# z of the softmax heads as seven block products of two by two, and six plain products moved in front of v

## The chip, the cores and the metric

The kernel runs on one core of a Trainium2 chip. The metric is the device time of one execution in microseconds; what is given is the median of several. A profiled execution is one single execution, with its own time.

## What is computed

The reference is one decoder layer on x of 512 rows and 1024 columns, all in float32. Cut to what matters here:

```python
h = rms_norm(x, norm_w)
qa, ka, va, za, qb, kb, vb, zb, gl_a, gl_b = split(h @ w_in)    # 8 of 512 columns, 2 of 1024
qa, ka = rms_norm(heads(qa), q_norm_w), rms_norm(heads(ka), k_norm_w)
oa = moba_attention(qa, ka, heads(va), rel_bias)                # softmax heads, branch a
ob = stick_breaking_attention(heads(qb), heads(kb), heads(vb))  # branch b
ya = (merge(oa) * silu(za)) @ w_up_moba
yb = (merge(ob) * silu(zb)) @ w_up_sb
y = sigmoid(gl_a + gb_a) * ya + sigmoid(gl_b + gb_b) * yb
x = x + y @ w_out
```

The z of the title is `za`, the gate path of the softmax heads; q and k are `qb` and `kb` of the stick-breaking heads; v is `va` and `vb` together.

## The kernel before

**Numbers.** Every large matrix product is made of three matmuls (`mm3`, L237): each operand is split into a rounded high part and the low remainder, and low times high, high times low and high times high are added up. Of a weight block of 128x1024 (512 KB), ScalarE writes the high part (L194) and VectorE the low part (L196); the raw block lies in one of three `wr` buffers, the parts in one of three `wh` and `wl` buffers. `load_w` (L157) hands out the next block of a fixed list, `stream` (L107), and keeps three of them ahead, so a block's split is written into the buffers of the block three before.

**Seven products in place of eight.** v, q and k (not z) are computed by a 2x2 block scheme of the Strassen-Winograd kind: x is cut into four quarters, and so are the weights; seven products of quarters give the result. For it some products take sums of x's quarters, S1 to S4 (`mix_x`, L368: VectorE sums, ScalarE high part, VectorE low part), and sums of the weights' blocks, T1 to T4 (`TERMS`, L38). Those sums are made by DMA: `load_sum` (L118) brings one block into a tile of the "v" pool, `add_sum` (L128) lets a DMA issued by POOL add a second block to it. T2 is T1 plus a block, T4 is T2 plus a block. The blocks "11", "21" and "22" are plain blocks that need no sum; by the list `ORDER` (L102) q and k take 11, T1, 21, T2, 22, T3, T4. The products of `columns` (L750) give q and k transposed, with matmuls of 256 columns; those of `values` (L701) give v, with matmuls of 512 columns, two blocks a product. PSUM banks X, D, Z, Y and E take the products; X collects several. Copies by ScalarE and sums by VectorE (L764) put the quarters of the result together.

**Order of the work around the change.** TensorE does, one after the other: qa; ka; `FRONT` (L46), that is a gate chunk g:0 and four z chunks (`f_z`, L640, `chunk_ct`, L505: 24 matmuls of 512 columns over one weight block); v; q; k; then the attention, in whose steps the list `FILLS` (L47) puts further gate, zb and up chunks. Beside the front, VectorE and ScalarE square and norm ka (`head_norm`, L401), spread qa and ka over the heads (`head_rows`, L415), turn them (`flip`, L437: eight VectorE transposes, eight DMAs by SP to memory), bring them back (`fetch`, L451: four DMAs by POOL), and split them inside v (`split_flipped`, L462).

**What sets the order.** A scheduler puts each engine's instructions into one fixed order, by the place in the program and by when it takes them to be ready; at run time each engine works through its order. `tc.issue_after(ins)` pins what follows on the engine of `ins` behind it, in order only. SP's and POOL's DMA issues are such orders too. Tiles of a pool are shared: "v" has 9 of 128x1024, "g" 31 of 128x512, PSUM has six banks "s" and two "pj".

Of the kernel before, what the change touches and what calls it, by code (L numbers as in the profile page):

```python
# [16 lines left out]
P = 128  # L17
# [28 lines left out]
FRONT = ("g:0", "za:0", "za:1", "za:2", "za:3")  # L46
# [13 lines left out]
def hybrid_layer(ctx: ExitStack, tc: tile.TileContext, x, xT, w, rel, out):  # L60
# [41 lines left out]
    ORDER = dict.fromkeys("qk", ("11", "T1", "21", "T2", "22", "T3", "T4"))  # L102
    ORDER["v"] = "11", "T1", "T2", "22", "T3", "21", "T4"
    HALVES = {"v": "ab", "q": ("",), "k": ("",)}
    BASE = {"v": 8, "q": 16, "k": 20}
    BLOCKS_OUT = [(kind, b + h) for kind in "vqk" for b in ORDER[kind] for h in HALVES[kind]]
    stream = list(range(8)) + list(range(24, 24 + len(FRONT))) + BLOCKS_OUT + list(range(24 + len(FRONT), WO)) + OUT  # L107

    def block(name, kind):
        if kind in "qk":  # L110
# [59 lines left out]

    def fetch_w(c):
        cuts = ((0, 512), (512, 1024)) if c < 2 else ((0, 1024),)
        item = stream[c]
        if item in sums:
# [62 lines left out]
    def mm3(ps, aH, aL, bH, bL, start, stop, on=False):  # L237

        with tc.issue_after(guard[0]) if guard[0] and start else nullcontext():
            T.matmul(ps, aH, bL, start=start, stop=False, skip_group_check=on)  # L240
# [127 lines left out]
    def mix_x(k):  # L368

        a, b = xraw[k], xraw[k + 4]  # L370
        left, right = slice(0, HS), slice(HS, S)
        V.tensor_tensor(b[:, right], a[:, right], b[:, right], op=ALU.subtract)
        V.tensor_tensor(a[:, right], a[:, left], a[:, right], op=ALU.subtract)
        V.tensor_tensor(a[:, left], b[:, right], a[:, left], op=ALU.subtract)
        V.tensor_tensor(b[:, left], b[:, left], a[:, left], op=ALU.add)
        h = tp.tile([P, 4 * PQ], F32R, tag="pt", bufs=4, name=f"mx{k}")
        if k < 2:
            l = tp.tile([P, 4 * PQ], F32R, tag="turned", bufs=2, name=f"ml{k}")
            l = [l[:, n * S:(n + 1) * S] for n in range(2)]
        else:  # L380
            l = [tp.tile([P, S], F32R, tag=("p3", "sx")[n], bufs=2, name=f"ml{k}{n}") for n in range(2)]
        for n, raw in enumerate((a, b)):
            hi, lo = h[:, n * S:(n + 1) * S], l[n]
            A.activation(hi, raw, AF.Copy)
            V.tensor_tensor(lo, raw, hi.bitcast(F32), op=ALU.subtract)
            for cs, name in ((left, ("S2", "S4")[n]), (right, ("S3", "S1")[n])):
                mixed[name, k] = hi[:, cs], lo[:, cs]
# [27 lines left out]
    def head_rows(ps, name, st):  # L415
        rows = []
        for t in range(NT):
            n = slot(f"{name}n{t}")
# [43 lines left out]
    def split_flipped(raws, name):  # L462

        res = []
        for p, raw in enumerate(raws):
# [18 lines left out]

    def spread(ps, name):
        with tc.issue_after(low[count[0] - 2]):
            rows = head_rows(ps, name, st[name])
        flipped[name] = flip(rows, name)

    flipped, raws = {}, {}  # L490
# [174 lines left out]

    for i, word in enumerate(FRONT):
        kind, n = word.split(":")
        f_g(int(n)) if kind == "g" else f_z("a", int(n))
        if i == 0:
            norm(ps_ka, "ka", after=summed[0])  # L670
            mix_x(0)
        elif i == 1:
            mix_x(1)
            summed.append(each(add_sum, "v", ("T3",), last["ka"]))
        elif i == 2:
            bring("qa")
            mix_x(2)
        elif i == 3:
            spread(ps_ka, "ka")
            mix_x(3)  # L680
        elif i == 4:
            bring("ka")
# [12 lines left out]
    s1, s2, s3, s4 = ([mixed[f"S{n}", k] for k in range(4)] for n in (1, 2, 3, 4))  # L695
# [5 lines left out]
    def values():  # L701
# [6 lines left out]
        X, W, Y = ([bank("s", f"v{n}{t}") for t in range(2)] for n in "xwy")  # L708
# [3 lines left out]
        product(W, s1, True)  # L712
        chain((load_sum, "q", "T1"), (add_sum, "q", "T1"))
        product(X, s2, False)
# [3 lines left out]
        chain((add_sum, "v", "T4"))  # L718
        for t in range(2):
            V.tensor_tensor(v_of["b"][t], W[t], top[t], op=ALU.subtract)  # L720
        qa.extend(split_flipped(raws["qa"], "qa"))
        product(Y, s4, True)
        for t in range(2):
            V.tensor_tensor(v_of["b"][t], Y[t], v_of["b"][t], op=ALU.add)
        product(X, s3, False)
        for t in range(2):
            A.activation(low_b[t], X[t], AF.Copy)
        for t in range(2):
            V.tensor_tensor(v_of["b"][2 + t], W[t], low_b[t], op=ALU.subtract)
        chain((load_sum, "q", "T2"), (add_sum, "q", "T2"), (load_sum, "q", "T3"), (add_sum, "q", "T3"))  # L730
        ka.extend(split_flipped(raws["ka"], "ka"))
        Z = [bank("s", f"vz{t}") for t in range(2)]
        product(Z, a12, True)
        for t in range(2):
            V.tensor_tensor(v_of["a"][t], Z[t], v_of["a"][t], op=ALU.add)
        product(X, a22, False)
# [6 lines left out]
    def product_ct(ps, a, start):  # L743
        hi, lo = load_w()
        for n in range(2):
            for k in range(4):
                ks = slice((2 * k + n) * P, (2 * k + n + 1) * P)
                mm3(ps[:, n * HS:(n + 1) * HS], hi[:, ks], lo[:, ks], *a[k], start and n + k == 0, k == 3, True)

    def columns(kind, c_of, steps):  # L750

        def quarter(c, r):
            return [c_of[2 * c + n][:, r * HS:(r + 1) * HS] for n in range(2)]

        def half_of(a, n):
            return a[n] if isinstance(a, list) else a[:, n * HS:(n + 1) * HS]

        def copy(ps, dst):
            for n in range(2):
                A.activation(dst[n], half_of(ps, n), AF.Copy)  # L760

        def add(dst, a, b, op=ALU.add):
            for n in range(2):
                V.tensor_tensor(dst[n], half_of(a, n), half_of(b, n), op=op)  # L764

        q11, q21, q12, q22 = (quarter(c, r) for c in range(2) for r in range(2))
        X, D, Z, Y, E = (bank("s", f"{kind}{n}") for n in "xdzye")
        product_ct(X, a11, True)
        copy(X, q11)
        product_ct(D, s1, True)  # L770
        copy(D, q22)
        steps[2]()
        product_ct(Z, a12, True)
        add(q11, Z, q11)
        product_ct(X, s2, False)
        add(q12, q22, X, ALU.subtract)
        steps[4]()
        product_ct(Y, s4, True)
        add(q12, Y, q12)
        product_ct(X, s3, False)  # L780
        add(q22, q22, X, ALU.subtract)
        copy(X, q21)
        steps[6]()
# [298 lines left out]
```

## Time and profile before

| what | us |
|---|---|
| median of 3 runs (382.64 to 383.13) | 382.86 |
| the profiled execution | 382.79 |
| its span, first to last instruction | 380.9 |
| VectorE busy, of the span | 292.2 |
| ScalarE busy, of the span | 216.8 |
| first z chunk to first matmul of v | 54.92 to 76.68 |
| v | 76.68 to 114.76 |
| q and k, to the first scores | 114.76 to 155.16 |

Times within the trace count from the span's start. PE is TensorE's matmuls, PEld its weight loads, DVE is VectorE, ACT is ScalarE, POOL is GpSimd and SP the engine that mostly issues DMAs. A row of the timeline gives start and duration, engine, line, the tiles written and read, and in brackets how long the engine was idle before it and what ended that. A row of a window gives the sum and, for each engine, the busy time in it; behind these stand TensorE's granted clock, the DMA engines' share and GB/s.

### The profile page before, as it was taken

How to read it: one execution, taken by the hardware profiler on the slowest of the kernel's cores; microseconds unless marked ns; L12 is line 12 of the kernel's file. 1: busy time of each engine (PE TensorE's matmuls, PEld its weight loads, DVE VectorE, ACT ScalarE, POOL GpSimd, SP SyncE). 2: the span in 40 equal slices, each digit the busy share in tenths (PEclk: the TensorE clock that was granted, in tenths of full speed). 3: DMA queues.
4: the chain of work that ended last, by engine and by line, in shares of the span. 5: the costliest groups of instructions: out<-in, count | busy, mean ns of one | idle time of the engine just before them, and what ended most of it. 6: DMA issues, size and time to landing. Idle time of an engine off the chain costs nothing.

```text
span 380.9 us, 5678 instructions
## 1 busy us (share of the span) xinstructions
PE 376.3 (99%) x2007; PEld 311.0 (82%) x2007; DVE 292.2 (77%) x505; ACT 216.8 (57%) x380; POOL 82.7 (22%) x125
## 2 busy tenths in 40 slices
PE   8999999999999999999999999999999999999996
PEld 5888888888889999888787878787878877888885
DVE  4828998975894656788885669599999717999962
ACT  5675655555875453799757464775464304368530
POOL 3859959213011020000000003001000000430310
PEclk9999999999999999999999999999999999999999
DMA  7989898989887994565998384959799853699964
GB/s 256 346 339 331 222 198 300 246 265 256 228 231 228 263 216 114 175 177 175 304 367 295 116 268 132 281 172 286 223 297 278 255 234 111 163 267 290 166 159 171
DMA packets 37611, 89.53 MB, mean 235 GB/s; under 512 B 4040, under 2 KB 16840, under 8 KB 37584
## 3 DMA queue, kind: packets, MB, share of 16 engines
q1 hardware_dynamic: 29856, 61.90, 47.8%
q0 software_dynamic: 6720, 23.09, 27.0%
q10 hardware_dynamic: 1008, 4.19, 3.2%
q8 instruction: 15, 0.25, 0.2%
q14 instruction: 12, 0.10, 0.1%
HBM read 70.27 MB, written 14.70 MB: 223 GB/s over the span
## 4 chain that ended last, share of the span: by engine, by line
PE 99%; DVE 0%; issue 0%
PE gl L240 8%; PE gl L242 8%; PE gl L241 8%; PE poa L627 2%; PE pob L627 2%; PE sb L525 2%; PE sa L525 2%; PE zb L240 2%; PE yb L240 2%; PE ka L240 2%; PE zb L241 2%; PE yb L242 2%; PE yb L241 2%; PE zb L242 2%; PE ya L240 2%; PE vx L242 2%
## 5 line engine op out<-in xcount | busy, mean ns | idle before, releaser
L196 DVE TENSOR_TENSOR wl<-wr,wh 128x1024 fp32r<-128x1024 f32 (+1 forms) x60 | 70.9, 1182 | 20.4 <-ACT wh L194 20.2
L194 ACT ACTIVATE wh<-wr 128x1024 fp32r<-128x1024 f32 (+1 forms) x60 | 61.7, 1030 | 24.6 <-issue 7.8
L240 PE MATMUL gl<-xl,wh 128*128 128x512 f32 x128 | 50.3, 393 | 0.0
L241 PE MATMUL gl<-xh,wl 128*128 128x512 f32 x128 | 49.8, 389 | 0.0
L242 PE MATMUL gl<-xh,wh 128*128 128x512 f32 x128 | 49.8, 389 | 0.0
L657 ACT ACTIVATE gl<-gl,x 128x512 f32<-128x512 f32 x16 | 10.9, 684 | 33.8 <-PE gl L242 33.8
L240 PEld LDWEIGHTS gl<-xl,wh 128*128 128x128 f32 x128 | 24.0, 188 | 5.3 <-ACT wh L194 0.2
L242 PEld LDWEIGHTS gl<-xh,wh 128*128 128x128 f32 x128 | 24.0, 188 | 5.1
L241 PEld LDWEIGHTS gl<-xh,wl 128*128 128x128 f32 x128 | 24.0, 188 | 4.9
L547 ACT ACTIVATE pa<-pa,m 128x512 f32<-128x512 f32 (+3 forms) x32 | 17.6, 551 | 8.3 <-DVE m L545 8.3
L146 POOL COPY turn_of<-pta 1x1 f32<-1x1 f32 x1 | 2.1, 2064 | 85.8 <-DVE sx L582 85.8
L572 DVE TENSOR_TENSOR_SCAN sx<-om,begin 128x512 f32<-128x512 f32 (+1 forms) x16 | 16.8, 1075 | 0.0
L594 DVE STREAM_TRANSPOSE turneda<-pa 128x384 f32<-128x384 f32 (+1 forms) x24 | 13.4, 600 | 2.2 <-ACT pa L552 2.0
L545 DVE CUSTOM_DVE_ANT_0 pa<-sa,om 128x512 f32<-128x512 f32 (+3 forms) x32 | 13.8, 483 | 0.6 <-DMA om<-e_dr 0.6
L594 DVE STREAM_TRANSPOSE turnedb<-pb 128x384 f32<-128x384 f32 (+1 forms) x24 | 12.9, 589 | 0.0
L240 PE MATMUL zb<-xl,wh 128*128 128x512 f32 x32 | 12.9, 404 | 0.0
L567 ACT ACTIVATE om<-sb 128x512 f32<-128x512 f32 (+1 forms) x16 | 8.9, 554 | 6.9 <-issue 6.9
L240 PE MATMUL yb<-olb,wh 128*128 128x512 f32 x32 | 12.6, 393 | 0.0
L241 PE MATMUL zb<-xh,wl 128*128 128x512 f32 x32 | 12.5, 391 | 0.0
L241 PE MATMUL yb<-ohb,wl 128*128 128x512 f32 x32 | 12.5, 390 | 0.0
L241 PE MATMUL ka<-wh,xl 128*128 128x512 f32 x32 | 12.5, 390 | 0.0
L240 PE MATMUL ka<-wl,xh 128*128 128x512 f32 x32 | 12.5, 390 | 0.0
(454 smaller groups left out, 1108.2 us busy)
## 6 DMA issues: line engine op xcount, KB each, us to landing
wr<-in_w SPq DMA_DIRECT2D x56, 512.0 KB, 5.2
pda<-turneda SPq DMA_DIRECT2D x32, 160.0 KB, 3.3
pta<-pda SPq DMA_DIRECT2D x8, 640.0 KB, 5.7
pdb<-turnedb SPq DMA_DIRECT2D x32, 160.0 KB, 4.4
ptb<-pdb ACTq DMA_DIRECT2D x6, 640.0 KB, 4.5
xn<-in_x SPq DMA_DIRECT2D x8, 256.0 KB, 6.1
om<-e_dr SPq DMA_DIRECT2D x8, 256.0 KB, 4.7
xr<-in_xT SPq DMA_DIRECT2D x7, 256.0 KB, 5.3
```

The source lines that it names most:

```text
L194: high[c] = A.activation(hi[:, a:b], raw[:, a:b], AF.Copy).ins
L196: low[c] = V.tensor_tensor(lo[:, a:b], raw[:, a:b], hi[:, a:b].bitcast(F32), op=ALU.subtract).ins
L240: T.matmul(ps, aH, bL, start=start, stop=False, skip_group_check=on)
L241: T.matmul(ps, aL, bH, start=False, stop=False, skip_group_check=on)
L242: end[0] = T.matmul(ps, aH, bH, start=False, stop=stop, skip_group_check=on).ins
L525: T.matmul(ps[b][:, c:c + n], x[o, i * P:(i + 1) * P], y[o, :n], start=m == 0, stop=m == 2)
L545: V.tensor_tensor_reduce(rows[i], sc[i], bias[:, S - n:], scale=1.0, scalar=3e38, op0=ALU.add, op1=ALU.min, accum_out=m[:, 0, i:i + 1])
L547: mark[0] = A.activation(rows[i], rows[i], AF.Exp, bias=m[:, 0, i:i + 1], scale=-1.0, accum_out=m[:, 1, i:i + 1]).ins
L572: V.tensor_tensor_scan(sx[:, n - 1::-1] if n == S else sx[:, :n][:, ::-1], om[:, S + 1 - n:][:, ::-1], begin[:, S - n:S][:, ::-1], 0.0, op ...
L594: turn_mark[0] = V.transpose(turned[:, :, at:at + n, :].rearrange("p q j r -> p j q r"), rows[i].rearrange("p (j q c) -> p j q c", j=n, q= ...
L627: guard[0] = T.matmul(po[o, :].rearrange("p (a n r) -> p a n r", a=4, r=32)[:, :, i:i + n, :], vv[j][:, c:c + HD], src, start=j == NT - 1, ...
L657: evicted.append(A.activation(g, ps, AF.Identity if raw[0] else AF.Sigmoid, bias=mb[:, i:i + 1]).ins)
```

## The change

- z is computed by `columns`, like q and k, from seven blocks; `FRONT` keeps g:0 alone. The weights' layout has z's quarters in place of its four chunks.
- The products of the plain blocks 11 and 21 of q, k and z (`plain_columns`) stand in front of v; X of each stays in its bank ("pj" for q and k, "s" for z) until the other five products, T1, T2, 22, T3 and T4, behind v, in the order z, q, k.
- T1 and T3 are still made by DMA; T2 and T4 are now made by VectorE in place, T1's tile plus a raw block (`made`). The raw block 22 that goes into T2 is kept for the product of 22.
- Raw blocks are called for two further ahead, from the front on (`early`), instead of from the attention on.
- ka is copied out of PSUM by ScalarE (`keep`); its spreading moves into v and its turning to z's second step, qa's turning into v, and bringing both back goes from POOL's queue to SP's; their splits move from v to q's and k's columns. W of v is copied out of PSUM.
- `mix_x` is cut into `mix_1`, `mix_23` and `mix_4`, placed behind the plain products and in v, each pinned behind a split on VectorE.
- z's gate (sigmoid, product) is made from the finished columns in q's steps (`z_gates`).

```diff
-FRONT = ("g:0", "za:0", "za:1", "za:2", "za:3")
+FRONT = ("g:0",)
...
-    ORDER = dict.fromkeys("qk", ("11", "T1", "21", "T2", "22", "T3", "T4"))
+    ORDER = dict.fromkeys("zqk", ("11", "T1", "21", "T2", "22", "T3", "T4"))
...
+    PLAIN = "11", "21"
+    BLOCKS_OUT = [(kind, b) for kind in "qkz" for b in PLAIN]
+    BLOCKS_OUT += [("v", b + h) for b in ORDER["v"] for h in "ab"]
+    BLOCKS_OUT += [(kind, b) for kind in "zqk" for b in ORDER[kind] if b not in PLAIN]
...
-        for c in range(count[0], count[0] + early[0]):
-            if c < len(stream) and c not in begun and isinstance(stream[c], int):
+        for c in range(count[0], min(count[0] + early[0], len(stream))):
+            src = source(stream[c])
+            if c not in begun and src is not None:
                 begun[c] = wp.tile([P, 1024], F32, tag="wr", bufs=3, name=f"wr{c}")
-                raw_dma[0] = nc.sync.dma_start(begun[c], w[stream[c]]).ins
+                raw_dma[0] = nc.sync.dma_start(begun[c], src).ins
...
+    def made(c):
+
+        kind, b = stream[c]
+        if b == "22":
+            return plain.pop(kind)
+        raw = begun.pop(c, None)
+        if raw is None:
+            raw = wp.tile([P, 1024], F32, tag="wr", bufs=3, name=f"wr{c}")
+            nc.sync.dma_start(raw, source(stream[c]))
+        if b == "T2":
+            plain[kind] = raw
+        t = sums[kind, "T1"]
+        V.tensor_tensor(t, t, raw, op=ALU.add)
+        return t
...
+    def mix_1(k):
 
         a, b = xraw[k], xraw[k + 4]
...
+        with tc.issue_after(low[count[0] - 2]):
+            V.tensor_tensor(b[:, right], a[:, right], b[:, right], op=ALU.subtract)
+        mix_part(k, 1, right, ((right, "S1"),))
...
-            with tc.issue_after(summed[-1]):
-                nc.gpsimd.dma_start(res[p], dr[p * P:(p + 1) * P, :])
+            with tc.issue_after(end[0]):
+                nc.sync.dma_start(res[p], dr[p * P:(p + 1) * P, :])
...
+    def keep(ps):
+
+        res = [slot(f"kac{t}") for t in range(NT)]
+        for t in range(NT):
+            A.activation(res[t], ps[t], AF.Copy)
+        return res
...
+    early[0] = 2
+    norm(ps_ka, "ka", after=summed[0])
+    ka_rows = keep(ps_ka)
+    f_g(0)
...
+    def plain_columns(kind, c_of, tag):
+
+        q11 = quarter(c_of, 0, 0)
+        X = held[kind] = bank(tag, f"{kind}x")
+        product_ct(X, a11, True)
+        copy(X, q11)
+        Z = bank("s", f"{kind}z")
+        product_ct(Z, a12, True)
+        add_to(q11, Z, q11)
...
+    plain_columns("q", q_raw, "pj")
+    mix_1(0)
+    mix_1(1)
+    plain_columns("k", k_raw, "pj")
+    mix_1(2)
+    mix_1(3)
+    mix_23(0)
+    summed.append(each(add_sum, "v", ("T3",), last["ka"]))
+    plain_columns("z", z_raw, "s")
+    mix_23(1)
+    mix_23(2)
+    mix_23(3)
...
+    columns("z", z_raw, {
+        1: lambda: (bring("qa"), flip_ka()),
+        2: lambda: chain((load_sum, "q", "T3"), (add_sum, "q", "T3")),
+        3: nothing,
+        4: lambda: chain((load_sum, "k", "T1"), (add_sum, "k", "T1"))})
     columns("q", q_raw, {
...
+        1: nothing,
+        2: lambda: (z_gates((0, 1)), qa.extend(split_flipped(raws["qa"][:2], "qa"))),
+        3: lambda: (z_gates((2, 3)), qa.extend(split_flipped(raws["qa"][2:], "qa", 2)), chain((load_sum, "k", "T3"), (add_sum, "k", "T3")), bring("ka")),
+        4: nothing})
+    columns("k", k_raw, {
+        1: nothing,
+        2: lambda: ka.extend(split_flipped(raws["ka"][:2], "ka")),
+        3: lambda: ka.extend(split_flipped(raws["ka"][2:], "ka", 2)),
+        4: nothing})
...
-    for c in range(2048, 3072, HS):
+    for c in [*range(2048, 3072, HS), *range(1536, 2048, HS)]:
```

More of the change, by code (lines that the diff above doesn't have):

```diff
@@ L169, in hybrid_layer, with source @@
     depth, behind = [3], [None]
+    def source(item):
+        if isinstance(item, int):
+            return w[item]
+        if not isinstance(item, tuple) or item in sums and item[0] == "v":
+            return None
+        kind, b = item
+        if kind == "v":
+            return None if b[0] == "T" else block(b, kind)
+        return {"T1": None, "T3": None, "T2": block("22", kind), "22": None,
+                "T4": block("21", kind)}.get(b, block(b, kind) if b[0] != "T" else None)
+    plain = {}
+    def made(c):
[11 more added lines that the diff above has]
+        return t
     def fetch_w(c):
@@ L366, in hybrid_layer @@
     mixed = {}
-    def mix_x(k):
-        a, b = xraw[k], xraw[k + 4]
-        left, right = slice(0, HS), slice(HS, S)
-        V.tensor_tensor(b[:, right], a[:, right], b[:, right], op=ALU.subtract)
-        V.tensor_tensor(a[:, right], a[:, left], a[:, right], op=ALU.subtract)
-        V.tensor_tensor(a[:, left], b[:, right], a[:, left], op=ALU.subtract)
[L375 to L387, printed above, removed]
+    left, right = slice(0, HS), slice(HS, S)
@@ L694, in hybrid_layer, with product_ct @@
     a22 = [(xH[k + 4][:, HS:], xL[k + 4][:, HS:]) for k in range(4)]
-    s1, s2, s3, s4 = ([mixed[f"S{n}", k] for k in range(4)] for n in (1, 2, 3, 4))
+    def product_ct(ps, a, start):
+        hi, lo = load_w()
+        for n in range(2):
+            for k in range(4):
+                ks = slice((2 * k + n) * P, (2 * k + n + 1) * P)
+                mm3(ps[:, n * HS:(n + 1) * HS], hi[:, ks], lo[:, ks], *a[k], start and n + k == 0, k == 3, True,
+                    None if n + k else end[0])
@@ new lines, in quarter, with half_of, copy, add_to @@
+    def quarter(c_of, c, r):
+        return [c_of[2 * c + n][:, r * HS:(r + 1) * HS] for n in range(2)]
+    def half_of(a, n):
+        return a[n] if isinstance(a, list) else a[:, n * HS:(n + 1) * HS]
+    def copy(ps, dst):
+        for n in range(2):
+            A.activation(dst[n], half_of(ps, n), AF.Copy)
+    def add_to(dst, a, b, op=ALU.add):
+        for n in range(2):
+            V.tensor_tensor(dst[n], half_of(a, n), half_of(b, n), op=op)
+    def mixes(n):
+        return [mixed[f"S{n}", k] for k in range(4)]
@@ new lines, in hybrid_layer, with columns @@
+    held = {}
+    def plain_columns(kind, c_of, tag):
[6 more added lines that the diff above has]
+        add_to(q11, Z, q11)
+    def columns(kind, c_of, steps):
+        q21, q12, q22 = (quarter(c_of, c, r) for c, r in ((0, 1), (1, 0), (1, 1)))
+        X = held[kind]
+        D, Y, E = (bank("s", f"{kind}{n}") for n in "dye")
+        product_ct(D, mixes(1), True)
+        copy(D, q22)
+        steps[1]()
+        product_ct(X, mixes(2), False)
+        add_to(q12, q22, X, ALU.subtract)
+        steps[2]()
+        product_ct(Y, mixes(4), True)
+        add_to(q12, Y, q12)
+        steps[3]()
+        product_ct(X, mixes(3), False)
+        add_to(q22, q22, X, ALU.subtract)
+        copy(X, q21)
+        steps[4]()
+        product_ct(E, a22, True)
+        add_to(q21, E, q21)
@@ L711, in values @@
             A.activation(v_of["a"][t], X[t], AF.Copy)
-        product(W, s1, True)
-        chain((load_sum, "q", "T1"), (add_sum, "q", "T1"))
-        product(X, s2, False)
+        for k in range(4):
+            mix_4(k)
+        W = [bank("s", f"vw{t}") for t in range(2)]
+        product(W, mixes(1), True)
+        wc = [slot(f"vwc{t}") for t in range(2)]
+        for t in range(2):
+            A.activation(wc[t], W[t], AF.Copy)
+        flipped["qa"] = flip(rows_of_head["qa"], "qa")
+        product(X, mixes(2), False)
         top, low_b = ([slot(f"v{n}{t}") for t in range(2)] for n in "bc")
@@ L741, in hybrid_layer @@
     v_of = values()
[L743 to L783, printed above, removed]
-        product_ct(E, a22, True)
-        add(q21, E, q21)
-        steps[7]()
@@ L788, in hybrid_layer, with nothing @@
[L788 to L795 removed]
+    def nothing():
+        pass
```

113 lines of the change are left out of this document (64 added, 49 removed).

## The prediction

> **What bounds the kernel now.** I read the page first, then the chain that ended last, then TensorE's waits, then the stages around the change.
>
> ```profile
> span 380.9 us, 5678 instructions
> PE 376.3 (99%) x2007; PEld 311.0 (82%) x2007; DVE 292.2 (77%) x505; ACT 216.8 (57%) x380; POOL 82.7 (22%) x125
> PEclk9999999999999999999999999999999999999999
> PE 99%; DVE 0%; issue 0%
> PE pwarm L230 <- DVE warm L88: 1.0, 1, 1.0
> ```
>
> TensorE is busy in 376.3 of 380.9 us, at nine tenths or more of its clock in every slice; the chain that ended last is TensorE to 99%, and its one wait is 1.0 us ahead of the first matmul. So the end is set by how many matmuls are issued and how far apart they stand; another engine counts only where it makes TensorE wait. The profiled execution took 382.79 us, 1.89 more than its span; the median of the runs is 382.86, so 0.07 is added to what I find for the one.
>
> **The change, part by part: TensorE.** Rows of matmuls (start, duration) at the borders of the stages:
>
> ```profile
> 54.92 0.39 PE L240 MATMUL za<-xl,wh 128*128 128x512 f32 x1
> 76.68 0.39 PE L240 MATMUL vx<-wl,xh 128*128 128x512 f32 x1
> 114.76 0.28 PE L240 MATMUL qx<-xl,wh 128*128 128x256 f32 x1
> 117.63 0.28 PE L240 MATMUL qd<-ml,wh 128*128 128x256 f32 x1
> 146.43 0.28 PE L240 MATMUL ky<-ml,wh 128*128 128x256 f32 x1
> ```
>
> Removed: four z chunks of 24 matmuls 512 wide, 76.68 - 54.92 = 21.76 us, 0.2267 each. Added: seven products of 24 matmuls 256 wide. Ten such products lie between qd and ky: 28.80 us, 2.88 each, 0.120 a matmul; seven are 20.16. An eighth of the multiplications goes (2.72 us of 21.76), but a matmul of half the width costs 53% of a full one, and **1.60 us** of it stay. The six plain products only change their place.
>
> [...]
>
> The new order, by these lengths: g:0 to 54.92; plain products of q, k and z to 72.20; v (114.76 - 76.68 = 38.08) to 110.28; five products of z to 124.68, of q to 139.08, of k to 153.48.
>
> **The weights' splits.** A block is split by ScalarE, then VectorE, into one of three pairs of buffers:
>
> ```profile
> 148.39 1.06 ACT L194 ACTIVATE wh<-kT 128x1024 fp32r<-128x1024 f32 x1 [3.36 <-DMA kT<-in_w]
> 149.48 1.23 DVE L196 TENSOR_TENSOR wl<-kT,wh 128x1024 fp32r<-128x1024 f32 x1 [2.09 <-ACT wh L194]
> 77.93 1.18 DVE L196 TENSOR_TENSOR wl<-wr,wh 128x1024 fp32r<-128x1024 f32 x1
> 79.40 0.39 PE L240 MATMUL vx<-wl,xh 128*128 128x512 f32 x1
> ```
>
> A split takes 2.3 us (148.39 to 150.71). A pair comes free when the product two places ahead of the block begins, so a block in the narrow products has 5.76 us for it: **3.5 us of slack**, against 8.6 behind a z chunk (2 x 5.44 - 2.3). That covers are thin already is seen at 77.93: this split ends at 79.11, and TensorE takes it up at 79.40, 0.3 later.
>
> **VectorE.** The stage before, and rows for its prices (busy us, mean ns, idle before):
>
> ```profile
> 49.64:76.46 26.82, 26.82 (x121) 22.19 (x120) 25.58 (x51) 14.84 (x21) 15.54 (x17) 1.00 0.97 257
> 110.50:154.00 43.50, 43.50 (x348) 42.76 (x347) 27.07 (x38) 20.98 (x31) 5.23 (x6) 1.00 0.79 196
> L196 DVE TENSOR_TENSOR wl<-wr,wh 128x1024 fp32r<-128x1024 f32 x8 | 9.8, 1223 | 5.8 <-ACT wh L194 5.8
> L196 DVE TENSOR_TENSOR wl<-kT,wh 128x1024 fp32r<-128x1024 f32 x4 | 4.9, 1225 | 5.7 <-ACT wh L194 5.7
> L196 DVE TENSOR_TENSOR wl<-qT,wh 128x1024 fp32r<-128x1024 f32 x4 | 4.9, 1224 | 2.4 <-ACT wh L194 2.4
> 123.59 0.76 DVE L764 TENSOR_TENSOR qb<-qz,qb 128x256 f32<-128x256 f32 x2
> L474 DVE TENSOR_TENSOR ka2l<-kaT,ka2h 128x512 fp32r<-128x512 f32 x1 | 0.7, 680 | 0.0
> L444 DVE STREAM_TRANSPOSE kat<-kan 128x256 f32<-128x256 f32 x5 | 1.7, 402 | 0.0
> 63.02 0.68 DVE L385 TENSOR_TENSOR ml<-xr,mx 128x512 fp32r<-128x512 f32 x1
> 63.62 0.68 DVE L644 TENSOR_TENSOR za<-za,za 128x512 f32<-128x512 f32 x1
> ```
>
> Behind v (110.28 to 153.48, 43.2 us) it gets: 15 splits at 1.22 = 18.3; sums T2 and T4 of three kinds; 4 pairs of block adds for each kind, 12 x 0.76 = 9.1; the gates' products 4 x 0.68 = 2.7; low parts of qa and ka, 8 x 0.68 = 5.4; ka's transposes 8 x 0.40 = 3.2. The weights' sum in place on VectorE is not in the trace: from below a pair of adds of a quarter each (0.76), from above the whole split with ScalarE's part (2.3); I take 1.22, the row with its shape and two SBUF inputs, 6 x 1.22 = 7.3. Together 46.0. Neighbours overlap by 0.08 (63.02 + 0.68 against 63.62), some 53 times, 4.2: **41.8 of 43.2 us, 97%**, where before 27.07 of 43.50 were busy. With 0.76 and 2.3 it would be 39 and 48.3.
>
> In front it is lighter: the stage before held 25.58 of 26.82 and TensorE never waited; qa's transposes (3.2), the ka rows and the z products (2.7 each) leave it; two or three splits, adds of q, k and z (3 x 0.76) and the cut mixes come in, beside products half as long. ScalarE gains three splits (3 x 1.06), copies of ka and of W (six) and of z's blocks; at 20.98 of 43.50 and 14.84 of 26.82 before, these lie beside VectorE's work and I cost them at nothing; were ScalarE late, the splits' slack would pay. The pins of the mixes queue them on VectorE behind a split, where only later mixes wait.
>
> **The sums' DMAs.** Rows are issues, with us to landing:
>
> ```profile
> qT<-in_w SPq DMA_DIRECT2D x3, 512.0 KB, 5.0
> qT<-in_w POOLq DMA_DIRECT2D x3, 512.0 KB, 5.2
> kT<-in_w SPq DMA_DIRECT2D x3, 512.0 KB, 5.9
> kT<-in_w POOLq DMA_DIRECT2D x3, 512.0 KB, 8.5
> kadr<-kat SPq DMA_DIRECT2D x8, 128.0 KB, 2.7
> ```
>
> Passes of 512 KB stay 24 (before 4 + 10 + 10, after 3 x 8), so I cost bandwidth at nothing. POOL issues 6 sums instead of 8, and the 8 fetches of qa and ka go over to SP, whose queue also carries raw blocks two further ahead; behind a waiting fetch on SP stand raw blocks and loads of sums. What gets thin is the chain of T3: a tile of the "v" pool (9, of which q's two and v's four stay held, so three rotate, and ka's two turned halves now ask for them too), a load by SP, an add by POOL, a split. By my order z's T3 tile is free at 116, ka's first half takes it until about 120.5 (1.6 of transposes, 2.7 of DMA), q's T3 loads to 125.5 and is added to 131 (5.0, 5.2; with k's rows 5.9 and 8.5 to 135). It is needed split at 133.32, so landed at 131.0. From both sides: early by some 2 us if the slots come sooner, late by 4. I take nothing, the nearest row being q's own.
>
> Sum: 382.79 - 1.60 = 381.2, as a median **381.3**.
>
> **The rivals.**
>
> A. The sums' DMAs take the place of the multiplications saved: T3 of q or k lands late and TensorE waits once or twice, 0.8 to 2.3 us in all. For it: the estimate above has no slack, and ScalarE waited 3.36 us on such a sum at 148.39. Against it: that wait never reached TensorE. At 1.5 us late: 382.8.
>
> [...]
>
> B. VectorE becomes the bound behind v, and the kernel gets slower. It has 43.2 - 41.8 = 1.4 us to spare and the splits' 3.5 once. Before, it stood idle there for ScalarE's part of splits 5.8 + 5.7 + 2.4 = 13.9 us. Up to 4.9 of such gaps cost nothing, at 6.5 the gain is gone; at two thirds of what there was, 9.3, TensorE waits 4.4 us: 381.3 + 4.4 = 385.7. Against it: qa's and ka's low parts, the gates and the transposes can fill gaps, and the later ones can slip behind the first scores.
>
> C. The front: the first plain product of q needs a "pj" bank, which ka's third tile holds until its square and its new copy are done.
>
> ```profile
> 48.76 1.74 DVE L444 STREAM_TRANSPOSE qat<-qan 128x256 f32<-128x256 f32 x5
> 54.48 1.19 ACT L405 ACTIVATE kasq<-ka 128x512 f32<-128x512 f32 x2 [3.21 <-DVE kast L406]
> ```
>
> That square began at 54.48, waiting for VectorE. Were it to stay there, square and copy (0.6 each) would end at 55.7 to 56.3, 0.8 to 1.4 behind 54.92: 382.4. Against it: the transposes ahead of those reductions are moved away, 3.2 us, so that about 2 us of slack come out.
>
> [...]
>
> **How the numbers follow.** A measurement of this kernel can tell about 0.2%, 0.77 us, from no change. TensorE stays covered, with waits under 0.8 us: 0.46, at 381.3. A 0.22 and C 0.07, at 382.8 and 382.4, within 0.2% (say 0.27 with both joined to smaller shifts, 0.02 going to faster). B 0.18, and A's far end (4 us late, 385.3) 0.06: slower. D 0.01. Faster 0.49, same 0.27, slower 0.24. The low end of the range is the forecast less 0.4 for jitter of covers and spacing, 380.9; above it takes in A, C, the near part of B and most of A's far end, to 384.6, and leaves out about 0.15.
>
> **What would show it.** Right: z's seven products 2.88 us each, v's 38.08 long, the first scores near 153.6, no TensorE wait but the first. A: TensorE waiting for a split of q's or k's T3 whose ScalarE part waited for a DMA. B: VectorE without idle time from 110 to 154, and TensorE waiting for low parts whose high parts were long done. C: a gap ahead of the first q product. The prediction is wrong if the waits behind v come to more than 0.8 us, or if the attention behind no longer stays covered when it starts 1.6 us earlier, which I take for unchanged.

## The result, and the profile after

The changed kernel takes **388.23 us** (median of 4 runs, 387.63 to 388.89) against 382.82 for the kernel before: a ratio of 1.0141, 95% interval 1.0123 to 1.0159. It is slower by 5.4 us where 1.6 less were forecast, and outside the range. The profiled execution took 388.06 us, its span is 386.3.

The page of the changed kernel, with the same rows as before: span, busy engines, TensorE's granted clock by slice, the chain that ended last.

```profile
span 386.3 us, 5864 instructions
PE 376.8 (98%) x2079; PEld 314.0 (81%) x2079; DVE 306.4 (79%) x528; ACT 224.3 (58%) x399; POOL 75.6 (20%) x115
PEclk9999999999999989999999999999999999999999
PE 97%; DVE 1%; issue 0%
```

TensorE is still the chain's engine, but one slice of the clock row now shows 8 (the 15th, 135 to 145 us). Its waits (line, what it waited for: us in all, times, longest), of which before had the last row alone:

```profile
PE qx L277 <- DVE wl L231: 1.9, 1, 1.9
PE qx L276 <- ACT wh L229: 1.4, 1, 1.4
PE vz L276 <- DVE wl L231: 1.3, 1, 1.3
PE pwarm L265 <- DVE warm L88: 1.0, 1, 1.0
```

Three waits are new: one in v's product Z, two in q's product on T3. What they cost is read from the first matmuls of the stages (start, duration); `gl` is g:0, `sa` the first scores.

```profile
49.17 0.39 PE L276 MATMUL gl<-xl,wh 128*128 128x512 f32 x1
...
111.96 0.28 PE L276 MATMUL zd<-ml,wh 128*128 128x256 f32 x1
...
126.35 0.28 PE L276 MATMUL qd<-ml,wh 128*128 128x256 f32 x1
...
160.37 0.50 PE L592 MATMUL sa<-ka0l,qa0h 64*128 64x512 f32 x2
```

z's five products take 126.35 - 111.96 = 14.39 us, 2.88 each, as forecast. But g:0 to the scores takes 111.20 us, where before took 105.68 (49.48 to 155.16) and 1.60 less would be 104.08. The 7.12 us too much are 0.34 in v's first products, 1.65 at vz, 1.61 before T3's first matmul, and 3.52 inside that product. Behind the scores nothing moved: 225.9 us to the end, 225.8 before.

**The wait at vz** (timeline; for SP, a row's second number is the time from the first issue of the group to the end of its last):

```profile
84.75 12.29 SPq L507 DMA_DIRECT2D qadr<-qat  x8
97.14 0.40 SPq L169 DMA_DIRECT2D wr<-in_w  x1
101.25 1.06 ACT L229 ACTIVATE wh<-wr 128x1024 fp32r<-128x1024 f32 x1 [1.02 <-DMA wr<-in_w]
102.34 1.23 DVE L231 TENSOR_TENSOR wl<-wr,wh 128x1024 fp32r<-128x1024 f32 x1 [1.39 <-PE vz L278]
103.62 0.50 PE L276 MATMUL vz<-wl,xh 128*128 128x512 f32 x1 [1.31 <-DVE wl L231]
```

Eight writes of qa's turned rows hold SP for 12.3 us. The raw block that vz needs stands behind them, leaves at 97.14, lands at 101.2, is split by 103.6, and TensorE takes it up at once.

**The wait at q's T3** (timeline of the same kernel):

```profile
116.07 5.73 SPq L507 DMA_DIRECT2D kadr<-kat  x7
121.89 0.42 SPq L126 DMA_DIRECT2D qT<-in_w  x1
...
123.84 2.29 SPq L517 DMA_DIRECT2D kaT<-kadr  x4
126.84 0.89 POOL L138 DMA_DIRECT2D qT<-in_w  x1 [20.04 <-DVE wl L231]
134.76 0.63 ACT L534 ACTIVATE qa3h<-qa 128x512 fp32r<-128x512 f32 x1
135.49 1.06 ACT L229 ACTIVATE wh<-qT 128x1024 fp32r<-128x1024 f32 x1
136.46 1.22 DVE L201 TENSOR_TENSOR qT<-qT,wr 128x1024 f32<-128x1024 f32 x1
137.59 2.50 DVE L231 TENSOR_TENSOR wl<-qT,wh 128x1024 fp32r<-128x1024 f32 x2
...
136.60 0.38 PE L276 MATMUL qx<-ml,wh 128*128 128x256 f32 x1 [1.45 <-ACT wh L229]
138.87 0.58 PE L277 MATMUL qx<-mx,wl 128*128 128x256 f32 x1 [1.88 <-DVE wl L231]
139.25 0.42 PE L278 MATMUL qx<-mx,wh 128*128 128x256 f32 x1
139.46 0.41 PE L276 MATMUL qx<-ml,wh 128*128 128x256 f32 x1
```

T3's load leaves SP at 121.89, behind seven writes of ka's rows; the adding transfer leaves POOL at 126.84 and needs 8.6 us, in company of ka's four fetches, to 135.5. With vz's delay in it, T3's product was due at 134.99 (136.60 - 1.61), so the sum would have had to land by about 132.7, the two splits taking 2.3 us. Three suspects meet there: the **transfer** (D), **ScalarE's queue** (S), whose last copy of qa ends at 135.4 too, and **VectorE's order** (V), which makes T4's sum at 136.46 ahead of T3's low part. When TensorE goes on, its matmuls stand 0.21 apart instead of 0.12, until 141.8: 1.37 us more. In all T3 costs 1.61 + 3.52 = 5.13 us: 1.61 for the high part, 2.15 for the low part (about 1.0 of it T4's sum ahead), 1.37 for the slow matmuls.

VectorE, the prediction's rival B (busy us of PE, PEld, DVE, ACT, POOL; clock, DMA share, GB/s, from z's first product to the scores):

```profile
111.96:160.37 48.41, 45.08 (x362) 44.54 (x361) 41.81 (x62) 28.80 (x45) 2.62 (x3) 0.96 0.72 209
```

It is busy 41.81 us, the sum that the prediction made (41.8), with 6.6 idle: not the bound.

### The profile page after: what moved, and what is told of

It is laid out like the page before. It is cut to its first block, busy times and chain, and to the rows that moved or that the text cites. A ratio compares the mean times of both kernels' runs of the same rounds, so it can differ in the third digit from the quotient of the medians.

```text
span 386.3 us, 5864 instructions
## 1 busy us (share of the span) xinstructions
PE 376.8 (98%) x2079; PEld 314.0 (81%) x2079; DVE 306.4 (79%) x528; ACT 224.3 (58%) x399; POOL 75.6 (20%) x115
## 4 chain that ended last, share of the span: by engine, by line
PE 97%; DVE 1%; issue 0%
PE gl L276 8%; PE gl L277 8%; PE gl L278 7%; PE poa L694 2%; PE pob L694 2%; PE sb L592 2%; PE sa L592 2%; PE zb L276 2%; PE vx L276 2%; PE yb L276 2%; PE zb L277 2%; PE yb L277 2%; PE ka L276 2%; PE vx L278 2%; PE ya L276 2%; PE ka L278 2%
## 5 line engine op out<-in xcount | busy, mean ns | idle before, releaser
L231 DVE TENSOR_TENSOR wl<-wr,wh 128x1024 fp32r<-128x1024 f32 (+1 forms) x59 | 69.8, 1184 | 17.8 <-ACT wh L229 16.1
L229 ACT ACTIVATE wh<-wr 128x1024 fp32r<-128x1024 f32 (+1 forms) x59 | 60.7, 1031 | 26.2 <-issue 8.2
L149 POOL COPY turn_of<-pta 1x1 f32<-1x1 f32 x1 | 0.3, 333 | 88.3 <-DMA pta<-pda 88.3
```

Of the source, the lines that this page charges most:

```text
L229: high[c] = A.activation(hi[:, a:b], raw[:, a:b], AF.Copy).ins
L231: low[c] = V.tensor_tensor(lo[:, a:b], raw[:, a:b], hi[:, a:b].bitcast(F32), op=ALU.subtract).ins
```

## The experiments

Ratios are to the kernel before, with 95% intervals. A gap is counted here from the start of one matmul to the start of the next, which is 0.12 us (256 wide) or 0.23 (512 wide) where TensorE doesn't wait; so counted, the changed kernel has 1.73 and 2.27 us at T3.

### Gates, queues, fetches

z's gates from steps 2 and 3 of q's stage to steps 1 and 4 of k's:

```diff
-        2: lambda: (z_gates((0, 1)), qa.extend(split_flipped(raws["qa"][:2], "qa"))),
+        2: lambda: qa.extend(split_flipped(raws["qa"][:2], "qa")),
...
     columns("k", k_raw, {
-        1: nothing,
+        1: lambda: z_gates((0, 1)),
```

> z's gates (four sigmoids, four products) move from q's steps 2 and 3 to k's steps 1 and 4. In the changed kernel TensorE waited 1.6 + 2.1 us at q's T3, whose high part ScalarE began at 135.49, right behind unbroken work since 125.5, while the sum of T3 landed at 135.44 (126.84 + 8.6). Theory S (ScalarE's queue): with 2.5 us of sigmoids gone the high part begins near 133, the wait shrinks to 1 us or less, 384 to 386 us. Theory D (the sum's DMA is late): the high part still begins near 135.4, now with idle time of ScalarE that ends with the DMA of q's T3; 388 us. Theory V (VectorE is full): 385 to 387, because four products of 0.68 leave the stretch too.

387.95 us, 1.0119 (1.0031 to 1.0208). The gap at T3 stays (1.78 and 1.62 us), and ScalarE in this run:

```profile
129.42 0.64 ACT L765 ACTIVATE qb<-qd 128x256 f32<-128x256 f32 x2
135.16 1.06 ACT L229 ACTIVATE wh<-qT 128x1024 fp32r<-128x1024 f32 x1 [5.10 <-DMA qT<-in_w]
```

It sits idle for 5.10 us until the transfer lands. So the transfer alone is enough to make T3 late. That doesn't clear ScalarE's queue in the changed kernel, where its work runs unbroken to 135.39. A new wait of 0.8 us comes at the first scores, for k's adds, which now stand behind the gates on VectorE.

Writes of turned rows on POOL's queue instead of SP's: qa's alone, then qa's and ka's.

```diff
-                nc.sync.dma_start(bass.AP(tensor=dr.tensor, ...
+                (G if name == "qa" else nc.sync).dma_start(bass.AP(tensor=dr.tensor, ...
```

> The eight writes of qa's turned halves go through POOL's queue in place of SP's, nothing else. They held SP from 84.75 to 97.14, and the raw block of v's second 21 half was issued only then and landed at 101.2; TensorE waited 1.6 us at 101.9. Theory Q (SP's queue): that raw block is issued before 90, the wait at v's Z is gone, 386.5 us; the wait at q's T3 stays as it is, 1.6 us earlier. Rival (the DMA engines are full there and would bring it late whatever the queue): the wait stays above 1 us and the time at 388.

> The writes of ka's turned halves go through POOL's queue as well as qa's, so that the load of q's T3 no longer stands behind them in SP's (it was issued at 121.89, behind eight writes from 113.77 to 121.8). Theory Q for v's wait as in the run before. Theory D for q's T3: load some 3 us sooner, sum landed near 131 to 133, wait 0 to 1.5 us, 382 to 385 us. Theory S: ScalarE reaches T3's high part near 134 after its other work all the same, wait still 3 us or more, 386.

389.44 us, 1.0158 (1.0114 to 1.0203), and 392.41, 1.0236 (1.0192 to 1.028). The wait at vz is gone in the first, so SP's hold made it. But POOL issues the adding transfers, and these now stand behind the writes: z's T1 add leaves at 99.7 (85.0 in the changed kernel), with new gaps of 0.84 in z's stage. In the second run q's T3 add leaves at 131.54 and TensorE waits 4.62 us, though POOL's last write was done by 130.2: the add waited for its load, forecast some 3 us sooner. With no write of ka's ahead of it on SP, that load left at 124.30, right behind the end of z's T4 low part (124.27), and landed at 130.9. So by the times it had waited for a tile that this low part still read. In the changed kernel the low part ends at 121.12 and the load leaves at 121.89: its place behind ka's writes cost it 0.8 us at most. In the first run the issue time saved on SP (the raw block of vz leaves at 87.58 there, not 97.14) is paid on POOL by z's T1 add.

ka's four fetches issued by POOL, behind k's T3 sum:

```diff
-            with tc.issue_after(end[0]):
-                nc.sync.dma_start(res[p], dr[p * P:(p + 1) * P, :])
+            with tc.issue_after(summed[-1] if name == "ka" else end[0]):
+                (G if name == "ka" else nc.sync).dma_start(res[p], dr[p * P:(p + 1) * P, :])
```

> ka is brought back by POOL, behind the sum of k's T3, in place of by SP, where its four fetches (1 MB) ran from 123.84 beside the sum of q's T3. Theory D, with the lateness from crowded DMA engines: the sum takes 5 to 6 us in place of 8.6, lands near 132.5, and the wait at q's T3 shrinks by 2 to 3 us: 385 to 386. Theory S: the high part still begins near 135.4 and the wait stays, 388. A new wait ahead of the first scores is possible in both, as ka arrives late.

390.27 us, 1.018 (1.0136 to 1.0224): gaps of 1.52 and 2.47 us stay at T3 and v's first products wait in addition. ScalarE's rows there:

```profile
136.63 0.63 ACT L534 ACTIVATE qa3h<-qa 128x512 fp32r<-128x512 f32 x1
137.17 1.04 ACT L229 ACTIVATE wh<-qT 128x1024 fp32r<-128x1024 f32 x1
```

Without the fetches beside it T3's add takes 5.7 us (128.91 to 134.6) in place of 8.6, so their company is worth about 3 us. But ScalarE, in unbroken work since 128.47, takes T3 up only at 137.17, 2.6 us after it has landed. So ScalarE's queue alone is enough for this wait too: in the changed kernel the two end within 0.1 us of each other, and curing either one leaves the other.

### T3's sum without the adding transfer

q's T3 as raw 22 plus raw 12 on VectorE, with the gates in q and in k:

```diff
+        if b == "T3":
+            V.tensor_tensor(raw, raw, plain.pop(kind), op=ALU.add)
+            return raw
...
-        2: lambda: chain((load_sum, "q", "T3"), (add_sum, "q", "T3")),
+        2: nothing,
```

> q's T3 is made like T2 and T4, by VectorE from two raw blocks (22, kept from T2, and 12, read plain), in place of by a load and an adding DMA; z's gates stay in q's steps. Moving the gates alone left ScalarE idle for 5.1 us until T3's sum landed at 135.2, so the DMA is one cause (theory D). Theory D alone: the wait of 1.7 + 2.3 us at q's T3 and the slow matmuls behind it go, 383 us. Theory D and S together (in the changed kernel ScalarE's queue ended at 135.39 and the sum landed at 135.44, so each hides the other): T3's high part still begins near 135 behind gates and qa, 386 to 388.

> q's T3 on VectorE and z's gates in k's steps. D alone, or D and S: no wait at q's T3, TensorE's granted clock stays at 1.00 there, and with v's Z still waiting 1.6 us the time is 383 to 384. Theory V (VectorE, with 1.2 us more work, is what bounds): a wait of 2 us or more stays in q's products.

389.3 us, 1.0167 (1.0146 to 1.0188), and 388.9, 1.0156 (1.0134 to 1.0179). Replacing the sum doesn't help: TensorE still waits 2.39 and 1.51 us in the one, 2.92 in the other. VectorE's sum has a queue of its own to stand in: in the second TensorE's wait is 2.5 us for the low part.

Then, on top of the second, qa's flip behind product Y of v instead of W; and on top of that, each sum that VectorE makes (T2 and T4 of z, q and k) pinned behind the low part of the block ahead of it. The first edit:

```diff
         product(W, mixes(1), True)
-        flipped["qa"] = flip(rows_of_head["qa"], "qa")
...
         product(Y, mixes(4), True)
+        flipped["qa"] = flip(rows_of_head["qa"], "qa")
```

> As the run before, and qa is turned behind v's Y in place of behind W, so that the raw blocks of 21 stand ahead of its eight writes in SP's queue. Theory Q: no wait at v's Z, TensorE waits under 1 us in all, 381.3 to 382.5. Rival (crowded DMA engines): the wait at Z stays over 1 us, 383 to 384.

> As the run before, and the sum of T4 is queued on VectorE behind the low part of T3, ahead of which it stood (1.1 us, at 136.46). Where T3 is no longer late it changes nothing beyond 0.2 us: 381.3 to 382.5; if the run before still waits at q's T3, 1 us less than that.

386.69 us, 1.01 (1.0085 to 1.0115): vz runs without a gap (5.47 us), so the flip's place is the cause of that wait. And 387.36, 1.0125 (1.0104 to 1.0145): the pin cuts T3's gap from 2.92 to 1.79, but gaps of 0.7 open at two other products, and nothing is won. The first was forecast at 381.3 to 382.5, the second 1 us below the first where T3 still waits.

### T3's sum left out

q's product on T3 takes raw 22 as it is, and qa's flip stands behind Y; the second run has z's gates in k's stage as well.

```diff
         if b == "22":
-            return plain.pop(kind)
+            return plain[kind] if kind == "q" else plain.pop(kind)
+        if b == "T3":
+            return plain.pop(kind)
...
-        2: lambda: chain((load_sum, "q", "T3"), (add_sum, "q", "T3")),
+        2: nothing,
```

> qa's flip stands behind product Y of v, and q's product on T3 takes the raw weights 22 as they are: the sum 22 + 12 of q is left out, its load and its adding transfer with it. z's gates stay in q's stage, as in the changed kernel. Theory D (the wait of q's T3 product, 1.61 + 3.52 us with its slow matmuls, is the late sum): no gap over 0.6 us at T3's product, none at vz, span 379.5 to 380.2, 381.3 to 382 us. Theory S (ScalarE's queue, held by z's gates and the copies of qa, makes T3's high part late by itself): a gap of 1 to 2.3 us stays there, and 383 to 385 us.

> As the run before, and z's gates moved from q's stage to steps 1 and 2 of k's: flip, sum and gates are all out of the way, with the same 84 fewer matmul-free stretches left to explain. If the waits found (vz, q's T3, the slow matmuls behind it) are the whole excess, TensorE from g:0 to the first scores takes 104.1 to 104.7 us and the kernel 381.0 to 381.8 us, as the prediction's arithmetic had it. If something else holds (a transfer behind them, the end of the kernel), a wait of 1 us or more comes up at another stage before the scores, or the gain is lost behind them, and it is 383 us or more.

382.85 us, 1.0001 (0.9984 to 1.0018), and 382.56, 0.9997 (0.9973 to 1.0021). The 5.4 us are gone with the two waits. In the first the gates stay in q, T3 is taken up without a gap, and only q's last product waits 0.9 us, at its second matmul. So gates in q's stage don't force a wait at T3. It doesn't clear ScalarE's queue, for its order is another there: T3's high part runs at 128.80, ahead of most of qa's copies, and in the changed kernel behind them all. TensorE's first matmuls of g:0 and of the scores in the second:

```profile
49.45 0.39 PE L278 MATMUL gl<-xl,wh 128*128 128x512 f32 x1
...
153.65 0.50 PE L594 MATMUL sa<-ka0l,qa0h 64*128 64x512 f32 x2
```

104.20 us, where the prediction's lengths give 104.08: **the 1.60 us are there once no block is late**. The run as a whole was forecast at 381.0 to 381.8 and came out higher, because the first scores take 1.06 us longer (3.11 to the next g chunk, 2.05 before) behind k's adds, late on VectorE behind the gates, as in the run with the gates in k's stage alone.

### The order on SP

Again nothing is left out. First ka's flip moved behind q's sums, into q's stage, with the gates in k's; then with the sums pinned:

```diff
-        1: lambda: (bring("qa"), flip_ka()),
-        2: lambda: chain((load_sum, "q", "T3"), (add_sum, "q", "T3")),
+        1: lambda: (bring("qa"), chain((load_sum, "q", "T3"), (add_sum, "q", "T3"))),
+        2: nothing,
...
     columns("q", q_raw, {
-        1: nothing,
+        1: flip_ka,
```

> Nothing is left out. qa's flip behind product Y of v; q's T3 sum chained at step 1 of z's stage in place of step 2, ahead of ka's flip, and ka's flip moved from step 1 of z's stage to step 1 of q's; z's gates in steps 1 and 2 of k's. Theory D with its cause on SP's queue (the load of T3 stood behind seven writes of ka's rows until 121.9): the load goes out before 117, the adding transfer lands before 128, no gap at q's T3, 381.2 to 382.5 us. Rival, crowding (the transfers are late whatever their place in the queue, and ka's rows are now the late ones): the adding transfer still takes over 8 us, or a wait of 1 us or more comes up at k's stage or the first scores, 383.5 to 386 us.

> As the run before, and VectorE's sums of T2 and T4 are pinned behind the low part of the block ahead of them, so that T4's sum cannot come before T3's low part. If VectorE's order is what is left (1.22 us of one sum), 0 to 1.2 us below the run before; if the sum is no longer late there, the same within 0.4 us.

391.59 us, 1.0223 (1.0199 to 1.0246), and 389.6, 1.0172 (1.0157 to 1.0187). The gap at q's T3 is 0.7 us at most. But k's T3, whose load in the first run leaves at 139.25 behind ka's eight writes (q's last low part ends at 135.5 there), makes TensorE wait 5.61 and 1.26 us, and 4.61 and 1.26 in the second. The wait has moved to the next sum behind the writes.

So only the two are exchanged: q's T3 at step 1 of z's stage, ka's flip at step 2; with the gates in k, with the gates in q, and with k's T3 on VectorE.

```diff
-        1: lambda: (bring("qa"), flip_ka()),
-        2: lambda: chain((load_sum, "q", "T3"), (add_sum, "q", "T3")),
+        1: lambda: (bring("qa"), chain((load_sum, "q", "T3"), (add_sum, "q", "T3"))),
+        2: flip_ka,
```

> Nothing is left out. qa's flip behind product Y of v; q's T3 sum chained at step 1 of z's stage, ka's flip one step later (step 2), so that only the order of the two on SP is exchanged against the changed kernel; z's gates all in step 1 of k's stage. Theory D-SP (the sum of T3 is late because its load stands behind ka's writes on SP): q's T3 load leaves before 110 and its adding transfer before 120, no gap at q's T3; ka's writes, about 6 us long, then stand ahead of k's T1 and T3 loads, which have till 141 and 147: 381.5 to 382.8 us. Rival C (the transfers between 110 and 140 don't fit whatever their order): a wait of over 1 us at k's T1 or T3 product in its place, and 384 to 387 us.

> As the run before, but z's gates stay in steps 2 and 3 of q's stage as in the changed kernel. The run in which T3's sum was left out had no wait at T3 with the gates in q, so theory D-SP expects the same as the run before, within 0.8 us. Theory S (ScalarE's queue) expects a wait of 1 us or more at q's T3 or its last product, with slow matmuls behind it, and 1.5 to 3 us above the run before.

> As e16, with z's gates in steps 1 and 2 of k's stage, and k's T3 as a sum of raw 22 and raw 12 on VectorE: two of the transfers in the crowded stretch become one, on a queue that adds nothing. If k's T3 is the late one in e16 this takes its wait away: 381.5 to 382.8 us. If k's T1 is the late one, or none, the same as e16 within 0.6 us, or up to 1.2 us above it where VectorE's 1.22 us sum stands ahead of an add that TensorE waits for.

387.53 us, 1.0114 (1.0089 to 1.0139); **383.87, 1.0021 (1.001 to 1.0032)**; 385.96, 1.0088 (1.0061 to 1.0116). The second is the best whole version: 4.4 us below the changed kernel, by the places of two flips and one sum alone. Its timeline (SP, POOL) and TensorE's waits:

```profile
104.05 0.33 SPq L126 DMA_DIRECT2D qT<-in_w  x1
...
118.30 6.22 SPq L507 DMA_DIRECT2D kadr<-kat  x8
126.19 0.35 SPq L126 DMA_DIRECT2D kT<-in_w  x1
...
134.01 2.15 SPq L517 DMA_DIRECT2D kaT<-kadr  x4
117.24 0.89 POOL L138 DMA_DIRECT2D qT<-in_w  x1 [9.90 <-DMA qT<-in_w]
130.26 0.88 POOL L138 DMA_DIRECT2D kT<-in_w  x1 [12.13 <-DVE qT L201]
```

```profile
PE kd L277 <- DVE wl L231: 0.7, 1, 0.7
PE kx L277 <- DVE wl L231: 0.7, 1, 0.7
PE qx L276 <- DVE qb L769: 0.4, 1, 0.4
```

T3's load leaves 17.8 us earlier than in the changed kernel, and q's only wait is 0.4, for q's adds. The exchange gives the load another, earlier tile along with its place ahead of the writes; the runs don't part the two. T3's high part runs at 127.96 on ScalarE, ahead of nearly all of qa's copies, so that cause is gone as well. What is late now is k's first sum, on T1: its load leaves at 126.19 behind the writes, it lands at 136.06, and ScalarE, with qa's copies and one for q's adds ahead of it, begins its high part at 138.33.

Theory S had the gates wrong way round: with them in k the kernel is 3.7 us slower, not faster. In both runs k's T1 add leaves POOL within half a microsecond (130.3 and 130.8). The first two fences (tile kT; time from issue to landing) are of the run with the gates in q and of that with them in k, the third is the timeline of the latter:

```profile
DMA to landing us min/median/max: 3.3/5.8/6.8
```

```profile
DMA to landing us min/median/max: 3.4/8.4/10.1
```

```profile
129.35 2.07 SPq L517 DMA_DIRECT2D kaT<-kadr  x4
140.92 1.06 ACT L229 ACTIVATE wh<-kT 128x1024 fp32r<-128x1024 f32 x1 [2.76 <-DMA kT<-in_w]
```

With the gates in k's stage, ka's fetches go out at 129.35 instead of 134.01, and k's T3 load at 128.98 instead of 133.13, into the add's time; it lands at about 140.9, 10.1 us after its issue (5.8 in the other run), and TensorE waits 2.76 and 1.26 us at k's D. So crowding shows in a second pair of traces, after 5.7 and 8.6 us for q's T3: transfers that are nobody's cause of delay in one order lengthen an adding transfer beside them in another (10.1 us against 5.8).

Two more orders, k's first load ahead of ka's writes too, and ka's writes last with k's T3 on VectorE:

```diff
-        2: flip_ka,
+        2: lambda: (chain((load_sum, "k", "T1"), (add_sum, "k", "T1")), flip_ka()),
```

> As e17 (qa's flip behind Y, q's T3 sum ahead of ka's flip, gates in q), and k's T1 sum is chained ahead of ka's flip too, at step 2 of z's stage in place of step 4. e17 lost 1.03 and 1.02 us at k's D and at its T1 product to the load of k's T1, which left at 126.2 behind ka's eight writes. Theory D-SP: the load leaves before 119, both gaps close, and 1.5 to 2.1 us are gained: 381.6 to 382.5 us. Rival C: ka's writes and k's T3 are late in their turn, a wait of 1 us or more at k's T3 or at the first scores, 383.5 us or more.

> As e14 (qa's flip behind Y, q's T3 sum at step 1 of z's stage, ka's flip in step 1 of q's stage), with z's gates in q's stage and k's T3 as a sum of raw 22 and raw 12 on VectorE, so that no weight sum's load is left behind ka's writes. Theory D-SP: the 5.6 us gap of e14 at k's T3 goes, 381.6 to 383 us. Rival C: raw 12 or the raw block of T4 is late behind ka's writes and fetches (133 to 143 us), a gap of 1 to 3 us at k's T3 or its last product, 384 to 386 us.

384.58 us, 1.0043 (1.0024 to 1.0061), and 387.19, 1.0125 (1.0094 to 1.0156): both misses for theory D in its simple form. In the first, k's T1 add leaves at 123.08 and k's D has no gap, but ka's second half of writes slips to 130.69, k's T3 load to 135.99, and TensorE waits 1.64 us at k's T3, 0.81 and 0.83 at two other products. In the second, whose runs scatter from 385.5 to 390.8, the profile has four gaps of 0.65 to 1.78 us, all in k's stage.

Last, the two moves of the best version parted: qa's flip behind Y, alone.

> The changed kernel with one edit: qa's flip behind product Y of v in place of product W. e17 holds this edit and the exchange of q's T3 sum with ka's flip; this run parts them. Theory Q (vz waited for a raw block that stood behind the flip's eight writes on SP): the 1.65 us at vz go and the wait at q's T3 stays (3 to 5 us with its slow matmuls), 386.0 to 387.0 us, so that the exchange alone is worth 2 to 3 us in e17. Rival: the two waits are one delay (what vz gives back, q's T3 takes, since its sum's load is bound to SP's time and not to TensorE's): 387.6 us or more.

387.46 us, 1.0111 (1.0078 to 1.0145). The time lies between the two forecasts. vz has no gap, and T3 keeps its whole wait:

```profile
PE qx L276 <- ACT wh L229: 2.1, 1, 2.1
PE qx L277 <- DVE wl L231: 1.2, 1, 1.2
```

By the ratios the first move is worth 0.3% (1.0141 to 1.0111, with intervals that overlap), by the two profiled executions 1.0 us; the exchange of q's T3 sum and ka's flip is worth 0.9% (1.0111 to 1.0021, intervals apart), some 3.4 us. The waits add up, less what v's first products vary by.

No version tried beats the kernel before. The best stands 0.2% above it, with 2 to 3 us of waits in q's and k's stages; the runs don't show whether an order exists in which every transfer of that stretch is in time.

## Why the prediction was wrong, point by point

**TensorE's arithmetic: right.** Seven products of 2.88 in place of 21.76 us, and v at 38.20 us (38.08 before) where no block is late; 104.20 measured against 104.08 where no block is late.

**The sums' DMAs: the step that failed.** The prediction worked out T3's chain with both ends, saw no slack at the near one and 4 us late at the far one, and wrote "I take nothing, the nearest row being q's own". The far end came true: the add needed 8.6 us (8.5 in k's rows, 5.2 in q's), landing at 135.5 where it had said "up to 135". It needed 131.0 by its timetable, and about 132.7 by that of the changed kernel, so it was 2.8 us late; with ScalarE's queue, which ends as late, and the slow matmuls the step cost 5.13 us. Its start was late as well, 126.84 against 125.5: the tile came free at 121.12, not about 120.5, and the place on SP behind ka's writes added up to 0.8. The rest is crowding: 5.7 us without ka's fetches beside the add, 8.6 with them. q's rows of before come from a stretch without ka's writes and fetches, which stood in v's stage (timeline of before, the writes):

```profile
76.73 5.70 SPq L446 DMA_DIRECT2D kadr<-kat  x8
```

The rows of the crowded k were the ones like the new stretch.

**SP's order: named, not priced.** "Behind a waiting fetch on SP stand raw blocks and loads of sums" is what happened at vz, only that the writes, not the fetches, held the queue. It cost 1.65 us, and the forecast had no term for it. "Passes of 512 KB stay 24, so I cost bandwidth at nothing" is true of the sum and says nothing of a place: what counted here is what was in flight beside the transfer that TensorE needed next (8.6 us with ka's fetches, 5.7 without).

**The price of a wait: too small.** The far end was priced at its 4 us (385.3); TensorE's slow matmuls behind the wait add 1.37.

**ScalarE at nothing: failed as well.** "I cost them at nothing" was said of its copies. Its queue is unbroken up to T3's high part at 135.49, and where the sum landed sooner (134.6, ka's fetches late) the high part began at 137.17. Where the sum is left out or early and the gates stay in q, ScalarE takes T3 up ahead of most of qa's copies (128.80, 127.96), and T3 doesn't wait. What was to be priced is where its queue stands when the block lands. **VectorE, rival B: right** in its sum, and it never became the bound; its order of instructions took a share (about 1.0 us at T3, T4's sum ahead of the low part) only after the transfer was late. **C** didn't occur: the first plain product of q follows g:0 without a gap. **D**, with its chance of 0.01, stands for shorter spacings, which no run shows: outside the slow stretch matmuls of 256 stood 0.120 apart (2.88 a product) and those of 512 0.227, as in the rows of before.

So rival A was the mechanism, T3's late block, at 5.1 us with the slow matmuls instead of 0.8 to 2.3, with the wait at vz on top. Its sign, a ScalarE part that waits for a DMA, doesn't show in the changed kernel, because ScalarE's own queue ended at the same moment; it shows with the gates in k (5.10 us). The chances gave its far end 0.06, though the estimate had no slack in it. And the forecast's own condition, waits behind v under 0.8 us, is what broke.

## What to carry to other kernels

A shared issue queue is a schedule: list, in order, everything that will stand on it in front of the load that the bound engine needs next, and price that load from the later of two times, the end of that list and the release of its tile. Then ask where the engine that splits it will be in its own queue when it lands: two causes that end together (within 0.1 us here) hide each other, and curing one alone gains nothing. When a chain has no slack by the estimate, take the duration from the stretch whose traffic is like the new one (8.5 us in k's rows, 8.6 measured), and carry the wait's consequences too (1.37 us of slow matmuls). If an edit moves small transfers into a stretch of back-to-back products, expect the late block to move when you reorder, as it did here from q's T3 to k's T1 and k's T3, and look for the order in the waits, one block at a time.

## What the runs showed of the hardware

**The waits at T3 cost more than themselves: 3.33 us of idle time, and 1.37 us of slow matmuls behind them.** After TensorE's waits at T3 (1.45 and 1.88 us with one matmul between) its matmuls of 256 stood 0.21 apart instead of 0.12 for 2.6 us; the granted clock of that stretch (138.4 to 141.8) is 0.50, and 1.00 ahead of it and behind it. In the twelve profiled executions with a wait of 2.5 us or more in all at one product, two waits with one matmul between counted together, the mean granted clock was 0.989 to 0.996; in the eight others, whose single waits reach 1.60 us, it was 0.998 to 1.00. In slices of 10 us the clock behind such a wait was 0.83 in one slice (q's T3 on VectorE), 0.91 and 0.92 in two (with the gates in k as well), 0.87 and 0.96 in two (qa's flip behind Y on top), which comes to 3.4 us at 0.50 in each of the three; behind a single wait of 1.9 us, at vz in the first of them, it was 1.00. After one of 1.60 us (the run with k's T3 on VectorE), at k's D, the spacing was back to 0.12 at the second matmul; after one of 2.54 (the run with qa's flip behind Y and T3 on VectorE) it was 0.12 at first and 0.21 from 137.46 on. The first fence is of the shorter wait, the second of the longer:

```profile
141.30 0.39 PE L282 MATMUL kd<-mx,wl 128*128 128x256 f32 x1 [1.60 <-DVE wl L236]
141.52 0.28 PE L283 MATMUL kd<-mx,wh 128*128 128x256 f32 x1
141.64 0.28 PE L281 MATMUL kd<-ml,wh 128*128 128x256 f32 x1
```

```profile
136.34 0.39 PE L282 MATMUL qx<-mx,wl 128*128 128x256 f32 x1 [2.54 <-DVE wl L236]
136.56 0.28 PE L283 MATMUL qx<-mx,wh 128*128 128x256 f32 x1
...
137.46 0.41 PE L281 MATMUL qx<-ml,wh 128*128 128x256 f32 x1
137.67 0.41 PE L282 MATMUL qx<-mx,wl 128*128 128x256 f32 x1
```

So a slow stretch came after an idle time as short as 2.54 us in one piece, and at a clock of 0.50 the spacing rose by 1.77 times (0.213 against 0.120), not 2. What sets its start and its length, no run shows.

**Writes of turned rows hold the issuing queue for very different times.** Eight of them took 12.3 us on SP at 84.75 in the changed kernel, all transposes being done by 86.0. With qa's flip behind Y, eight of qa's took 6.5 us where nothing else was changed, and 6.0 to 6.2 in three runs with q's T3 sum ahead of ka's flip (gates in k, gates in q, k's T3 on VectorE), while a single load of four times the bytes (512 KB against 128) took 0.33 to 0.43 in the changed kernel. What sets that time isn't settled.
